# Low halves of split fp32 weights: an accumulating DMA in place of a VectorE subtraction, in a two-layer streaming encoder

## The chip, the cores and the metric

The kernel runs on one core of a Trainium2 chip. The metric is device time in microseconds (us) of one execution, as the median of several runs of the same program; less is better. Engines are called PE (TensorE), DVE (VectorE), ACT (ScalarE), POOL (GpSimd) and SP (SyncE, which only issues DMAs here). PEld is the weight load of TensorE.

## The reference

One step of an encoder with two layers, on 560 tokens (32 sample tokens, 16 meta tokens, 512 prompt tokens) of width 1024. Cut to what matters:

```python
def mixer_inputs(x, pos, lp):
    h = rmsnorm(x, lp["norm_g"])
    proj = jnp.einsum("btd,de->bte", h, lp["w_in"])      # 1024 -> 4688
    q, k, v, z_a, qi, ki, wi, u, v_m, o_m, z_m, ig, fg = split_cols(proj)
    ...

def layer_output(x, attn, z_a, h_m, c, o_m, z_m, lp):
    hn = rmsnorm(h_m, lp["head_norm_g"])
    branch_m = (jax.nn.sigmoid(o_m) * hn + lp["skip"] * c) * jax.nn.silu(z_m)
    branch_a = attn * jax.nn.silu(z_a)
    mixed = jnp.concatenate([branch_a, branch_m], axis=-1)
    return x + jnp.einsum("bte,ed->btd", mixed, lp["w_out"])
```

Between the two projections stand a sparse attention (an indexer scores all keys, the 128 best of a row are kept, 8 heads of 64 attend) and a chunkwise mLSTM (4 heads of 128, fed by a causal convolution). All is fp32, and the choice of the best keys makes it sensitive to the precision of the projections.

## The kernel before, in words

To reach fp32 precision with the faster fp32r matmul, each operand is split into a high half (the value rounded to fp32r) and a low half (the rest). A product is three matmuls: high by high, low by high, high by low.

The weights of a layer come in pieces of 128 or 256 columns, named by what they make: I and KI (indexer), U (convolution input), M (mLSTM values), Q, K, V, O, Z, G (gates), Y (output). `load_piece` brings one in as tiles of 128 x 512: two tiles for a piece of 128 columns, four for M and V, whose pieces have 256 columns. For each tile it issues a DMA from DRAM into `wraw` on SP's queue, copies that into the high half `whi` (on ACT, DVE or POOL, by the option `wh..`), and subtracts to get the low half `wlo` (DVE with option `wl..` 0, POOL with 2, by turns with 1). There are 180 tiles in the two layers; there are 3 buffers of `wraw` and 5 each of `whi` and `wlo`, used in turn, so tile n waits until the matmuls of tile n-5 have read theirs.

`mm_feat` multiplies a piece of 128 columns with all 560 tokens in two parts (304 and 256 columns); `mm_tok` does M and V, five blocks of tokens one after the other (blocks 4, 0, 1, 2, 3), each going through all four tiles. So the four tiles of an M or V piece come free only within its last block, and the next piece begins right after.

Instructions are emitted in the order of the lists `STEPS`, under priorities (`PR`, `SHIFT`), and a list scheduler that keeps its own estimate of time places them in each engine's queue. Every engine then works through its queue strictly in order: an instruction that waits holds up all behind it. POOL also does rotary products, convolution sums, the sums of squares at the start, small normaliser chains and a third of the softmax work; in the tables below its line L639 is the sum of squares and L641 and L642 the copies of the sample and meta tokens' columns.

The numbered lines in the profile belong to the kernel before: L490 is every plain DMA, L476 every copy by ACT, L513 the subtraction. `dap` describes a region of DRAM; the weights `w` stay there unchanged.

Of the kernel before, what the change touches and what calls it, by code (L numbers as in the profile page):

```python
# [9 lines left out]
F32 = mybir.dt.float32  # L10
# [4 lines left out]
OP = mybir.AluOpType  # L15

P = 128
# [33 lines left out]
WOFF = {}  # L51
# [4 lines left out]
WTOT = _o  # L56
# [381 lines left out]
def body(ctx, tc, nc, d):  # L438
# [6 lines left out]
    def T(tag, shape, dt=F32, name=None):  # L445
        tag = swap.get(tag, tag)
        cnt[tag] = cnt.get(tag, 0) + 1
        return pool.tile(shape, dt, tag=tag, bufs=BUFS.get(tag, 1), name=name or f"{tag}_{cnt[tag]}")
# [24 lines left out]
    act, dve, gps, pe = nc.scalar, nc.vector, nc.gpsimd, nc.tensor  # L473

    def acopy(out, in_, scale=1.0):
        return act.activation(out, in_, AF.Copy, scale=scale)  # L476
# [4 lines left out]
    def copy(site, l, out, in_, scale=1.0):  # L481
        o = OPT[f"{site}{l}"]
        if o == 0:
            return acopy(out, in_, scale)
        if isinstance(scale, float) and scale == 1.0:
            return (dve, gps)[o - 1].tensor_copy(out, in_)
        return (dve, gps)[o - 1].tensor_scalar(out, in_, scale, None, op0=OP.mult)

    def dma(out, in_):
        return nc.sync.dma_start(out, in_)  # L490

    def dap(t, off, ap):
        return bass.AP(tensor=t.tensor, offset=t.offset + off, ap=ap)
# [8 lines left out]
    def load_piece(l, name, base=1000):  # L502
        w = WIDTH[name]
        kk = 512 // w
        his, los = [], []
        with prio(l * 1000000 + base):
            for q in range(KT // kk):
                cut = lambda t: t[:, :kk * w].rearrange("p (k e) -> p k e", k=kk)
                raw, hi, lo = cut(T("wraw", [P, 512])), cut(T("whi", [P, 512], F32R)), cut(T("wlo", [P, 512], F32R))
                dma(raw, dap(d["w"], l * P * WTOT + WOFF[name] + q * kk * w, [[WTOT, P], [w, kk], [1, w]]))  # L510
                copy("wh" + name[0], l, hi, raw)
                o = OPT[f"wl{name[0]}{l}"]
                (gps if o == 2 or (o == 1 and q % 2) else dve).tensor_tensor(lo, raw, hi.bitcast(F32), op=OP.subtract)  # L513
                his.append(hi)
                los.append(lo)
        wtiles[l, name] = his, los, kk
# [144 lines left out]
    def layer(l, x_in, sums):  # L661
# [14 lines left out]
        for n in ("I0", "I1", "KI", "I2", "I3")[2 * (l == 0):]:  # L676
            load_piece(l, n)
# [207 lines left out]
        def conv(m):  # L885
            load_piece(l, f"U{m}")
            with prio(B + PR[l]["U"] + off[0]):
                u = T("gt", [P, 566])
                dma(u[:, 0:3], d["conv_in"][l, :, m, :])
                gps.memset(u[:, 35:38], 0.0)  # L890
                ps, ps1 = mm_feat(l, f"U{m}")
                with prio(B + PR[l]["D"]):
                    acopy(u[:, 3:35], ps[:, 0:32])
                    acopy(u[:, 38:310], ps[:, 32:304])
                    acopy(u[:, 310:566], ps1)
                gps.tensor_tensor(u[:, 3:35], u[:, 3:35], rrow[:, 0:32], op=OP.mult)
                E("us", l).tensor_tensor(u[:, 38:566], u[:, 38:566], rrow[:, 32:560], op=OP.mult)
                dma(d["sample_conv"][l, :, m, :], u[:, 32:35])
                dma(d["prompt_conv"][l, :, m, :], u[:, 563:566])
                y = T("gt", [P, 566])  # L900
                act.activation(y[:, :563], u[:, 0:563], AF.Identity, bias=sml[:, 16 + m:17 + m],
                               scale=sml[:, 4 * m:4 * m + 1])
                for i in range(1, 4):
                    if OPT[f"ut{i}{l}"]:
                        dve.scalar_tensor_tensor(y[:, :563], u[:, i:i + 563], sml[:, 4 * m + i:4 * m + i + 1], y[:, :563],
                                                 op0=OP.mult, op1=OP.add)
                        continue
                    tap = T("gt", [P, 566])
                    acopy(tap[:, :563], u[:, i:i + 563], sml[:, 4 * m + i:4 * m + i + 1])
                    gps.tensor_tensor(y[:, :563], y[:, :563], tap[:, :563], op=OP.add)  # L910
                act.activation(u[:, 0:563], y[:, :563], AF.Tanh, scale=0.5)
                dve.scalar_tensor_tensor(c2[:, m, 0:32], u[:, 0:32], 1.0, y[:, 0:32], op0=OP.add, op1=OP.mult)
                dve.scalar_tensor_tensor(c2[:, m, 32:560], u[:, 35:563], 1.0, y[:, 35:563], op0=OP.add, op1=OP.mult)
                dma(c2scr[l, m], c2[:, m, :])
# [3 lines left out]
        def proj_m(c):  # L918
            load_piece(l, f"M{c}")
            for j in ORDER:  # L920
                if c == 0:
                    v1[j] = T("v4" if j == 4 else "tok", [P, NTOK])[:, :516].rearrange("p (h e) -> p h e", e=129)
                    gps.memset(v1[j][:, :, 128:129], 1.0)
                mm_tok(l, f"M{c}", j, v1[j][:ROWS[j], 2 * c:2 * c + 2, 0:128], rc)
# [498 lines left out]
```

## Time and profile before

| what | value |
|---|---|
| median of 3 runs | 936.02 us (934.91 to 940.69) |
| the profiled execution's own time | 936.46 us |
| its span in the trace | 934.7 us |
| busy share PE / DVE / ACT / POOL | 92% / 79% / 46% / 51% |
| DMA: share of the 16 engines' time | 37% |
| mean granted TensorE clock | 0.968 |

Busy times are unions of an engine's instructions; DMA issues and waits are not counted in them. The chain that ended last is found by going back from the last instruction to whatever released it. Windows are stretches of the execution in us from the start of the span.

### The profile page before, as it was taken

To read this page: it belongs to the slowest core of one execution; us is meant where nothing else is said; L and a number is where in the kernel's file an instruction comes from. 1 tells how busy PE (TensorE), PEld (TensorE's weight loads), DVE (VectorE), ACT (ScalarE), POOL (GpSimd) and SP (SyncE) were. 2 spreads that over 40 slices of the span, in tenths; PEclk is the share of its full clock that TensorE was granted. 3 is DMA by queue.
4 is the path that set the end of the run, shared out by engine and by line. 5 is a ranking of instruction groups with operands and counts; after the bars stand their busy time and mean duration, and the time that the engine had idled before them with its cause. 6 is when DMAs were issued, how large, how long until landed. Compare 5 with 4: busy or idle time off the path is not lost.

```text
span 934.7 us, 18526 instructions
## 1 busy us (share of the span) xinstructions
PE 859.5 (92%) x6446; PEld 794.6 (85%) x6446; DVE 738.7 (79%) x1790; ACT 425.4 (46%) x1081; POOL 478.2 (51%) x825
## 2 busy tenths in 40 slices
PE   6877989999999999979999678999799999999998
PEld 5876889899888989858999667998699889888898
DVE  7699999899996865865757998898899886887531
ACT  5346735465555442454323666333355453243410
POOL 8466552474502223452824855248577765656411
PEclk9997999999999999979999979999799999999999
DMA  7432224443553232332643411334334642332152
GB/s 227 117 82 66 59 73 145 107 111 106 164 170 104 69 96 81 88 94 68 202 118 93 98 47 60 93 114 120 94 91 142 191 115 82 96 109 76 57 177 76
DMA packets 82158, 99.98 MB, mean 107 GB/s; under 512 B 16720, under 2 KB 44192, under 8 KB 82064
## 3 DMA queue, kind: packets, MB, share of 16 engines
q1 hardware_dynamic: 82064, 98.79, 37.0%
q8 instruction: 51, 0.84, 0.4%
q14 instruction: 43, 0.35, 0.1%
HBM read 72.19 MB, written 15.21 MB: 94 GB/s over the span
## 4 chain that ended last, share of the span: by engine, by line
PE 51%; DVE 24%; POOL 6%; DMA 6%; issue 6%; ACT 4%; SPq 2%; DVEq 0%; ACTq 0%; POOLq 0%
PE pj L559 10%; PE pj L561 10%; PE pj L560 10%; PE pv L1208 3%; DVE wlo L513 3%; PE sc L1171 2%; DVE wk L826 2%; SPq L490 2%; PE tp L1197 2%; DVE m L825 2%; PE pj L535 2%; PE pj L537 2%; PE pj L536 1%; PE pv L1209 1%; DMA fx<-kscr 1%
## 5 line engine op out<-in xcount | busy, mean ns | idle before, releaser
L559 PE MATMUL pj<-h,whi 128*128 128x304 f32 (+3 forms) x548 | 165.8, 305 | 14.9 <-ACT h L476 5.2
L561 PE MATMUL pj<-h,whi 128*128 128x256 f32 (+3 forms) x548 | 163.8, 301 | 2.7 <-DVE h L629 2.7
L560 PE MATMUL pj<-h,wlo 128*128 128x304 f32 (+3 forms) x548 | 163.5, 299 | 0.0
L476 ACT ACTIVATE whi<-wraw 128x512 fp32r<-128x512 f32 x130 | 80.2, 626 | 106.5 <-PE pj L561 63.4
L513 DVE TENSOR_TENSOR wlo<-wraw,whi 128x512 fp32r<-128x512 f32 x136 | 103.9, 768 | 26.7 <-ACT whi L476 26.3
L559 PEld LDWEIGHTS pj<-h,whi 128*128 128x128 f32 (+1 forms) x548 | 105.8, 194 | 19.4 <-ACT h L476 5.2
L561 PEld LDWEIGHTS pj<-h,whi 128*128 128x128 f32 (+1 forms) x548 | 105.4, 193 | 6.4 <-DVE h L629 5.0
L560 PEld LDWEIGHTS pj<-h,wlo 128*128 128x128 f32 (+1 forms) x548 | 106.1, 194 | 1.2 <-issue 0.8
L559 PE MATMUL pj<-at,whi 128*128 128x304 f32 (+2 forms) x346 | 104.8, 303 | 1.7 <-ACT tok L476 0.8
L561 PE MATMUL pj<-at,whi 128*128 128x304 f32 (+2 forms) x346 | 103.1, 299 | 0.0
L560 PE MATMUL pj<-at,wlo 128*128 128x304 f32 (+2 forms) x346 | 102.8, 297 | 0.0
L513 POOL TENSOR_TENSOR wlo<-wraw,whi 128x512 fp32r<-128x512 f32 x44 | 58.5, 1334 | 59.3 <-ACT whi L476 41.3
L559 PEld LDWEIGHTS pj<-at,whi 128*128 128x128 f32 (+1 forms) x346 | 66.6, 193 | 3.1 <-ACT tok L476 1.1
L825 DVE MAX8 m<-wk 96x8 f32<-96x560 f32 (+3 forms) x120 | 67.6, 563 | 1.6
L561 PEld LDWEIGHTS pj<-at,whi 128*128 128x128 f32 (+1 forms) x346 | 66.5, 192 | 0.6 <-issue 0.5
L560 PEld LDWEIGHTS pj<-at,wlo 128*128 128x128 f32 (+1 forms) x346 | 66.8, 193 | 0.1
L826 DVE MATCH_REPLACE8 wk<-m,wk 96x560 f32<-96x560 f32 (+3 forms) x120 | 65.8, 548 | 0.0
L1183 ACT ACTIVATE lg<-lg,sta,ssq 128x528 f32<-128x528 f32 (+3 forms) x64 | 42.4, 663 | 39.0 <-DVE sta L1182 35.9
L559 PE MATMUL pj<-tok,whi 128*128 128x304 f32 (+3 forms) x188 | 55.9, 297 | 0.0
L560 PE MATMUL pj<-tok,wlo 128*128 128x304 f32 (+3 forms) x188 | 55.6, 296 | 0.0
L561 PE MATMUL pj<-tok,whi 128*128 128x304 f32 (+3 forms) x188 | 55.4, 295 | 0.0
L1276 DVE TENSOR_TENSOR m<-pj,fr 128x304 f32<-128x304 f32 (+1 forms) x28 | 12.6, 449 | 45.7 <-PE pj L561 43.2
(386 smaller groups left out, 2584.9 us busy)
## 6 DMA issues: line engine op xcount, KB each, us to landing
wraw<-w SPq DMA_DIRECT2D x176, 256.0 KB, 2.8
fx<-fr SPq DMA_DIRECT2D x68, 70.0 KB, 2.5
m<-scratch SPq DMA_DIRECT2D x16, 256.0 KB, 4.0
fx<-tok SPq DMA_DIRECT2D x32, 70.0 KB, 2.4
c2scr<-ca SPq DMA_DIRECT2D x8, 280.0 KB, 2.2
k_out<-fr SPq DMA_DIRECT2D x8, 280.0 KB
gt<-c2scr SPq DMA_DIRECT2D x8, 280.0 KB, 2.6
m<-hmscr SPq DMA_DIRECT2D x8, 280.0 KB, 3.1
```

The lines of the kernel that those rows point to most:

```text
L476: return act.activation(out, in_, AF.Copy, scale=scale)
L490: return nc.sync.dma_start(out, in_)
L513: (gps if o == 2 or (o == 1 and q % 2) else dve).tensor_tensor(lo, raw, hi.bitcast(F32), op=OP.subtract)
L535: pe.matmul(ps[:R, :256], hh, wh, start=first, stop=False)
L537: pe.matmul(ps[:R, :256], hl, wh, start=False, stop=last)
L559: pe.matmul(o, wh, hh, start=(i == 0 and j == 0), stop=False)
L560: pe.matmul(o, wl, hh, start=False, stop=False)
L561: pe.matmul(o, wh, hl, start=False, stop=(i == 1 and j == 3))
L825: dve.max(m8[:R], src)
L826: dve.match_replace(out=wk[:R, :S], in_to_replace=m8[:R], in_values=src, imm_value=NEG)
L1183: act.activation(lg[:R, :S], lg[:R, :S], AF.Exp, bias=st[:R, 2:3], scale=qs, accum_out=st[:R, 3:4])
L1208: pe.matmul(o[s], vt[i][:, hs], pts[s][:, i * P:(i + 1) * P], start=(i == 0), stop=False)
```

## The change

For tiles whose low half DVE formed, the kernel now has ACT write the negated high half into `wlo`, and POOL then issue a DMA that reads the weights from DRAM a second time and adds them onto it in SBUF. Tiles whose low half POOL formed stay as they were. The lines behind the edit move down by 5.

```diff
@@ -507,10 +507,15 @@
             for q in range(KT // kk):
                 cut = lambda t: t[:, :kk * w].rearrange("p (k e) -> p k e", k=kk)
                 raw, hi, lo = cut(T("wraw", [P, 512])), cut(T("whi", [P, 512], F32R)), cut(T("wlo", [P, 512], F32R))
-                dma(raw, dap(d["w"], l * P * WTOT + WOFF[name] + q * kk * w, [[WTOT, P], [w, kk], [1, w]]))
+                src = dap(d["w"], l * P * WTOT + WOFF[name] + q * kk * w, [[WTOT, P], [w, kk], [1, w]])
+                dma(raw, src)
                 copy("wh" + name[0], l, hi, raw)
                 o = OPT[f"wl{name[0]}{l}"]
-                (gps if o == 2 or (o == 1 and q % 2) else dve).tensor_tensor(lo, raw, hi.bitcast(F32), op=OP.subtract)
+                if o == 2 or (o == 1 and q % 2):
+                    gps.tensor_tensor(lo, raw, hi.bitcast(F32), op=OP.subtract)
+                else:
+                    acopy(lo, hi.bitcast(F32), -1.0)
+                    gps.dma_start(out=lo, in_=src, accum_op=OP.add)
                 his.append(hi)
                 los.append(lo)
         wtiles[l, name] = his, los, kk
```

The scheduler sees other instructions, and its order moves on all engines. Three places follow; numbers behind a tile's name count the tiles of that name (the second is the compiler's own).

The first is POOL's queue at the start of the program, while the first indexer piece is loaded. Before:

```order
L639 TENSOR_TENSOR fx_1_123<-fx_1_123,lg_1_149 128x304
L641 COPY hc_1_140<-h_3_126 128x48
L642 COPY hc_1_140<-h_2_125 128x48
L642 COPY hc_1_140<-h_4_127 128x48
L641 COPY hc_1_140<-h_5_128 128x48
L639 TENSOR_TENSOR fx_1_123<-fx_1_123,lg_2_156 128x304
```

The same place after:

```order
L644 TENSOR_TENSOR fx_1_127<-fx_1_127,lg_1_153 128x304
L647 COPY hc_1_144<-h_2_129 128x48
L518 DMA wlo_1_86<-w 128x512
L644 TENSOR_TENSOR fx_1_127<-fx_1_127,lg_2_160 128x304
L646 COPY hc_1_144<-h_3_130 128x48
L647 COPY hc_1_144<-h_4_131 128x48
L646 COPY hc_1_144<-h_5_132 128x48
L518 DMA wlo_2_93<-w 128x512
```

The DMAs for the first two low halves stand between the sums of squares; PE's second matmul reads `wlo_1`.

The second is ACT's queue at the second M piece of the first layer, tiles 25 to 28 (`whi_26` needs the buffer of tile 21, which belongs to the first M piece). Before:

```order
L476 ACTIVATE whi_26_1797<-wraw_26_1796 128x512
L911 ACTIVATE gt_16_1365<-gt_17_1425 128x563
L476 ACTIVATE whi_27_1803<-wraw_27_1802 128x512
L476 ACTIVATE whi_28_1809<-wraw_28_1808 128x512
L476 ACTIVATE tok_8_1762<-pj_25_1764,smn_2_411 128x2x128
```

The same place after:

```order
L476 ACTIVATE whi_26_1822<-wraw_26_1821 128x512
L940 ACTIVATE m2_16_1511<-m2_16_1511,ta_1_681 48x48 x4
L886 ACTIVATE te_1_682<-tp_9_1500 48x8
L476 ACTIVATE whi_27_1829<-wraw_27_1828 128x512
L476 ACTIVATE wlo_26_1823<-whi_26_1822 128x512
L916 ACTIVATE gt_16_1385<-gt_17_1445 128x563
L476 ACTIVATE whi_28_1836<-wraw_28_1835 128x512
L476 ACTIVATE wlo_27_1830<-whi_27_1829 128x512
L476 ACTIVATE tok_8_1786<-pj_25_1788,smn_2_421 128x2x128
```

The negated copy into `wlo_26` stands behind four exponentials (L940), a small one and the next high half.

The third is POOL's queue at the same piece. Before:

```order
L910 TENSOR_TENSOR gt_17_1425<-gt_17_1425,gt_20_1433 128x563
L1051 TENSOR_TENSOR smk_2_1312<-smk_2_1312,smn_2_411 128x10
L543 TENSOR_SCALAR v4_1_1656<-v4_1_1656,smn_2_411 48x2x128
L486 COPY at_16_1345<-at_14_1337 64x48
L486 COPY at_16_1345<-at_15_1338 64x48
```

The same place after:

```order
L915 TENSOR_TENSOR gt_17_1445<-gt_17_1445,gt_20_1453 128x563
L518 DMA wlo_26_1823<-w 128x512
L518 DMA wlo_27_1830<-w 128x512
L518 DMA wlo_28_1837<-w 128x512
L518 DMA wlo_29_2025<-w 128x512
L486 COPY at_16_1363<-at_14_1355 64x48
L486 COPY at_16_1363<-at_15_1356 64x48
```

Four DMAs follow each other; the copies of the first keys and all of POOL's later work stand behind them.

On PE, between the last matmul that reads tile 21 and the first that reads `wlo_26`, stood 24 matmuls before; now 41 stand there.

## Rows read from the trace of the kernel before

**Rows 1.** Busy time, and shares of the chain that ended last (two rows of the page).

```profile
PE 859.5 (92%) x6446; PEld 794.6 (85%) x6446; DVE 738.7 (79%) x1790; ACT 425.4 (46%) x1081; POOL 478.2 (51%) x825
...
PE 51%; DVE 24%; POOL 6%; DMA 6%; issue 6%; ACT 4%; SPq 2%; DVEq 0%; ACTq 0%; POOLq 0%
```

**Rows 2.** Windows: stretch, length, busy us of each engine, clock, DMA share, GB/s.

```profile
0.00:23.00 23.00, 15.11 (x54) 12.71 (x55) 18.02 (x30) 12.15 (x25) 19.71 (x49) 1.00 0.75 230
...
47.00:117.00 70.00, 57.12 (x381) 50.67 (x380) 67.43 (x98) 44.28 (x95) 43.91 (x56) 0.93 0.26 69
117.00:260.00 143.00, 136.58 (x1088) 129.55 (x1086) 132.07 (x375) 74.34 (x206) 72.23 (x148) 0.98 0.43 121
...
515.00:585.00 70.00, 54.09 (x342) 48.01 (x341) 65.16 (x104) 44.77 (x97) 44.56 (x56) 0.90 0.26 68
...
796.00:913.00 117.00, 113.15 (x884) 104.10 (x883) 76.41 (x215) 40.80 (x101) 57.45 (x90) 1.00 0.34 102
```

**Rows 3.** The same windows, the subtraction L513 alone: DVE, then POOL.

```profile
47.00:117.00 70.00, 9.31 (x12) 0.00 (x0) 0.93 0.26 69
...
515.00:585.00 70.00, 8.95 (x10) 0.00 (x0) 0.90 0.26 68
```

**Rows 4.** Groups: line engine op out<-in, form, xcount | busy us, mean ns | idle before.

```profile
L476 ACT ACTIVATE whi<-wraw 128x512 fp32r<-128x512 f32 x130 | 80.2, 626 | 106.5 <-PE pj L561 63.4
L513 DVE TENSOR_TENSOR wlo<-wraw,whi 128x512 fp32r<-128x512 f32 x136 | 103.9, 768 | 26.7 <-ACT whi L476 26.3
...
L513 POOL TENSOR_TENSOR wlo<-wraw,whi 128x512 fp32r<-128x512 f32 x44 | 58.5, 1334 | 59.3 <-ACT whi L476 41.3
```

**Rows 5.** Tile view of `wlo`: who waited for it (us, times).

```profile
  PEld pj L532: 0.9, 2
...
  PE pj L532: 0.5, 2
```

**Rows 6.** Timeline at the start: start, us, engine, line, form.

```profile
4.70 0.69 DVE L513 TENSOR_TENSOR wlo<-wraw,whi 128x512 fp32r<-128x512 f32 x1 [4.70 <-ACT whi L476]
...
5.16 0.62 PE L559 MATMUL pj<-h,whi 128*128 128x304 f32 x1 [5.16 <-ACT h L476]
...
5.58 0.49 PE L560 MATMUL pj<-h,wlo 128*128 128x304 f32 x1
...
6.32 0.96 POOL L639 TENSOR_TENSOR fx<-fx,lg 128x304 f32<-128x304 f32 x1 [0.67 <-ACT h L476]
...
7.23 0.47 POOL L641 CAST hc<-h 128x48 fp32r<-128x48 f32 x1
```

**Rows 7.** DMAs: one weight tile's issue on SP (ns min/median/max), KB and us to landing.

```profile
L490 SPq DMA_DIRECT2D wraw<-w x180: 327/334/1377, 1.2 to 908.5; - x180
...
DMA to landing us min/median/max: 2.5/2.8/4.5
...
m<-scratch SPq DMA_DIRECT2D x16, 256.0 KB, 4.0
...
q1 hardware_dynamic: 82064, 98.79, 37.0%
```

**Rows 8.** Timelines of PE and ACT at the first layer's M pieces.

```profile
121.12 0.32 PE L532 MATMUL pj<-wlo,hc 128*48 128x256 f32 x1 [0.30 <-DVE wlo L513]
...
135.25 0.28 PE L536 MATMUL pj<-wlo,h 128*128 128x256 f32 x1
...
138.16 0.36 PE L532 MATMUL pj<-wlo,hc 128*48 128x256 f32 x1
...
135.33 0.63 ACT L476 ACTIVATE whi<-wraw 128x512 fp32r<-128x512 f32 x1 [0.22 <-PE pj L537]
...
140.99 1.01 ACT L935 ACTIVATE m<-m,ta 48x48 f32<-48x48 f32 x4
```

**Rows 9.** One short POOL copy in the stretches where DVE is full (ns min/median/max).

```profile
L756 POOL CAST at<-at x8: 209/722/776, 67.4 to 86.0; 128x32 fp32r<-128x32 f32 x8
```

## The prediction

> **What bounds the kernel now.** I read the page's busy shares and chain first, then the windows by stage, then the views of the low halves. PE is busy 92% of the span and carries half of the chain, DVE a quarter, POOL 6% [rows 1]. So the most that any change off PE can win is PE's idle time, 934.7 - 859.5 = 75 us. The windows show where it lies [rows 2]: in most stages PE works nearly all the time (113.2 of 117 us at 796 to 913), but in the two stretches where indexer scores and convolutions are made, at 47 to 117 and 515 to 585, PE idles 12.9 and 15.9 us while DVE works 67.4 and 65.2 of 70. There DVE is the bound, with ACT and POOL at 63% each. At the start PE idles 7.9 us of 23, waiting for input. At 117 to 260 PE (136.6 of 143) and DVE (132.1) are both near full.
>
> The low halves are not what PE waits for: in the whole run its projections and their weight loads waited for `wlo` 1.4 us [rows 5]. ACT's high halves wait for PE instead, 63.4 us in all [rows 4]: weights are prepared ahead, and a free buffer sets when.
>
> **The change part by part.** All sums are against the profiled execution, 936.46 us, which is 0.4 us above the median.
>
> Removed: 136 subtractions on DVE, 103.9 us [rows 4], of which 9.3 and 9.0 us lie in the two stretches that DVE bounds [rows 3]. The other 86 us lie beside a busy PE or in stages where both are near full.
>
> Added on ACT: 136 copies of the size of the high half's, 626 ns each [rows 4], 85 us. ACT goes from 425 to 510 us of 935, no bound by itself.
>
> Added on POOL: 136 DMA issues. No DMA is issued there before, so the trace has no price. SP's issue of the same tile takes 0.33 us [rows 7]; POOL's own subtraction of it 1.33 us [rows 4]. I take 1.0, nearer to POOL's row, because the work is done on POOL: 136 us, and POOL goes from 478 to about 614 us.
>
> Added on the DMA engines: 35 MB read again. The one queue moved 98.8 MB in 37.0% of the engines' time [rows 7], so 35 MB are 13 points, 26 if the destination is read as well. No stage but the first (75% busy [rows 2]) comes near full, so I cost the traffic at nothing there and count it in the landing. A plain tile lands 2.8 us after its issue, 4.5 at most, and the transfer of 256 KB with rereads takes 4.0 [rows 7]; I take 4.0, since this DMA handles its bytes twice. So from when POOL reaches the DMA to a usable low half I count 1.0 + 4.0 = 5 us, bounds 0.33 + 2.8 = 3.1 and 1.33 + 4.5 = 5.8, where one subtraction of 0.77 stood.
>
> *Where this is hidden.* In a piece of 128 columns a tile feeds 24 matmuls, one every 0.12 us [rows 8], some 3 us. With five buffers a tile is needed four tiles after its buffer came free, 11 us and more. High half, negation and DMA need 0.63 + 0.63 + 5 = 6.3 us. That cover costs nothing while the queues of ACT and POOL are prompt; without it each such tile would cost up to 5 us. No DMA tiles stand in layer 0's Y pieces (all on POOL); in layer 1's, POOL's half is used first.
>
> *The start: +4 us* (1 to 7). PE's second matmul reads the first low half at 5.58, right behind the subtraction at 4.70 to 5.39 [rows 6]. After, the order puts the DMA on POOL behind a sum of squares, which starts at 6.32 and takes 0.96, and a copy of 0.47 [rows 6]: reached at 7.8, landed at 12.8, so PE, in order, is 7.2 us late. It catches up what it idled there after its first matmul, 2.7 us of the 7.9 (its first matmul starts at 5.16 [rows 6]).
>
> *The M and V pieces: +12 us* (4 to 25). Their four tiles are freed only in the piece's last block of tokens, so the cover is thin. Before, the fourth tile of M0 was late already: PE waited for its subtraction [rows 8]. Tile 21 is read for the last time at 135.25, and `wlo_26` for the first time at 138.16 [rows 8]: 2.9 us for 24 matmuls. The scheduler has put 41 there now, 41 x 0.12 = 4.9 us. Against this stand, in ACT's new order, the high half 0.63, four exponentials 1.01 [rows 8], the next high half 0.63, the negation 0.63, and then 5 us: 7.9, and 8.3 with the small instruction and a start 0.1 us after the release. PE is short by 3.4 us. At M0's last tile, where 43 matmuls give 5.0 us and nothing stands between, it needs 0.63 + 0.63 + 5 = 6.3 and is short by 1.3. There are six such places (last tile of M0, M1 and V1, in each layer). I take 2 each, between the two: 12. With 3.1 us for the DMA they would nearly vanish; at 5.8 and a busier queue they double.
>
> *The stretches that DVE bounds: -10 us* (-20 to +5). At most 9.3 + 9.0 = 18.3 us go, and a couple more at 117 to 260. But 22 negations and DMAs go into the 140 us: ACT from 89 to 103 us, POOL from 88.5 to 110.5 [rows 2], and both stand in order, POOL behind waits for ACT. POOL's sums feed the convolution and the rotary products that DVE waits for. I let half of the gain through. The gain on DVE's sharing with POOL is unpriced and inside this range.
>
> *POOL's queue elsewhere: +7 us* (0 to 20). A DMA there waits for ACT's negation, and everything behind it waits too: the key copies and mLSTM products behind `wlo_26` to `wlo_29`, the small normaliser chains. The 44 subtractions on POOL already waited 41.3 us for the high half [rows 4], 0.94 each; at that rate 136 DMAs hold POOL 136 x 1.94 = 264 us, 28% of the time. The chain has 6% on POOL [rows 1], 56 us or some 40 pieces of 1.4; if each meets a held queue 28 times in 100 for half of 1.94 us, that is 11 us, of which I let 7 reach the end. Below nothing I see no mechanism.
>
> Sum: 936.5 + 4 + 12 - 10 + 7 = 949.5; I say 949, 1.4% slower.
>
> **What a page adds.** POOL's copy of 128 x 32 takes 209 ns at best and 722 in the median where DVE is full [rows 9]: POOL's work stretches 3.5 times there. The Trainium skill, page "SBUF — State Buffer", section "SBUF: two separate sides", says why this could strike the new DMAs: descriptors of a DMA issued from GpSimd are written by GpSimd's own cores, which are locked out while VectorE runs a copy in a mode that takes the port they share. Row and rule point the same way, against the change; no run here shows it for a DMA yet. It is the third rival below, whose price comes from the row.
>
> **The rivals.**
> Faster: the DMA is usable 3.1 us after POOL reaches it and DVE's relief comes through. The start costs 1, the six places 0.5 each, POOL's queue 2, the stretches give 20: 936.5 + 1 + 3 + 2 - 20 = 922. For it speaks that DVE is full there at 96% and 93% [rows 2]; against it, that POOL and ACT take up as much work as DVE loses. It decides where the first term in DVE's place (POOL) stays under some 75% busy there.
>
> No change: other matmuls fill the six places, as the order tries, and POOL's hold-ups fall where it idles: 936.5 + 4 + 3 - 10 + 3 = 937.
>
> Much slower: POOL becomes the bound in the two stretches. If an issue there stretches 3.5 times, 22 x 3.5 = 77 us join the 88.5 that POOL works: 165 of 140, so +25 in place of -10, and the M and V places, with issues 2.5 us later, cost 2.5 each more: 949.5 + 35 + 15 = 1000; with half of the stretching, 975. I price it at 982.
>
> The change doesn't do it: the DMA's rounding or form could make the compiler add instructions. The order shows 136 DMAs on POOL and no others, so 2 in 100, at about 949 too.
>
> **How the numbers follow.** Chances: forecast 0.46 (its own range 939 to 965), no change 0.24, faster 0.14, much slower 0.14, the last 0.02. The range of 8 in 10 must cut into both ends: 926 leaves about a tenth below, 976 a tenth above. A change within 1% (927.1 to 945.8 by the profiled time) can't be told from none. Faster: 0.12 of the rival and 0.01 of the no-change case, 0.13. Slower: the forecast's part above 945.8, 0.35, and 0.14, and 0.01 of the last: 0.50. The rest, 0.37, is the same.
>
> **What would show it.** Right: POOL gains 136 issues of about 1 us, DVE's busy time falls by some 100 us and ACT's rises by 85; PE's second matmul moves from 5.6 to 11 or later; PE's waits for a DMA onto `wlo` add up to 10 to 25 us, nearly all in M and V pieces; PE stays without such waits at 796 to 913. The two stretches shrink by less than 10 us together. Wrong: landing over 7 us, so that plain pieces wait too; an issue on POOL of 2 us or more; or DVE's stretches shrinking by their full 18 us. The weakest numbers are the two that no row prices, issue and landing: 1 us in their sum moves the M and V places by 6 us and POOL's queue by several.

## The result, and the profile after

The changed kernel takes 994.15 us (median of 4 runs, 992.53 to 1001.41) against 937.47 for the kernel before beside it: a ratio of 1.0616, 95% interval 1.0572 to 1.0661. The direction was as forecast; 949 us and the range up to 976 were not. The profiled execution took 1001.41 us, with a span of 999.6.

The page of the changed kernel, its rows on busy time, the two DMA queues (packets, MB, share of the engines' time) and the chain:

```profile
PE 879.6 (88%) x6446; PEld 814.8 (82%) x6446; DVE 665.5 (67%) x1654; ACT 499.6 (50%) x1217; POOL 567.0 (57%) x961
...
q1 hardware_dynamic: 82064, 98.79, 33.9%
q0 software_dynamic: 19584, 35.50, 22.9%
...
PE 53%; DVE 16%; DMA 13%; POOL 5%; issue 5%; ACT 4%; SPq 3%; DVEq 0%; POOLq 0%; ACTq 0%
```

Beside [rows 1], DVE has lost 73 us of busy time, ACT gained 74 and POOL 89. (POOL's 136 issues are counted as busy here, 961 instructions being 825 and 136; its other instructions take 471 us.) PE idles 120.0 us of the span (999.6 - 879.6) where it idled 75.2, and the same 6446 matmuls keep it busy 20.1 us longer: 44.8 + 20.1 are the 64.9 us by which the span grew. In the chain DVE's share fell by 8 points and DMA's rose from 6% to 13%; POOL's, which is where the new instructions stand, went down a point. That row misleads, as will be seen.

The new instructions, grouped (line engine op out<-in xcount | busy us, mean ns | idle before):

```profile
L518 POOL DMA_DIRECT2D wlo<-w x136 | 125.6, 957 | 107.6 <-ACT wlo L476 64.0
...
L476 ACT ACTIVATE wlo<-whi 128x512 fp32r<-128x512 f32 x136 | 84.0, 623 | 22.5 <-DVE whi L486 18.8
```

An issue takes 0.96 us, as assumed. But POOL also stands idle 107.6 us right before them, 64.0 of it for ACT's negation. The step holds the head of POOL's queue for 125.6 + 107.6 = 233 us.

The tile view of `wlo` after (first the groups, then who waited, us and times):

```profile
L565 PE MATMUL pj<-h,wlo x548: 276/297/622, 14.6 to 502.8; 128*128 128x304 f32 x89, 128*128 128x256 f32 x89, 128*108 128x256 f32 x3, 128*108 128x304 f32 x2
...
L518 POOL DMA_DIRECT2D wlo<-w x136: 589/884/1748, 7.8 to 979.4; - x136
...
  PE pj L565: 11.5, 2
...
  PE pj L537: 8.4, 8
...
DMA to landing us min/median/max: 3.8/4.9/9.2
```

POOL reaches the first DMA at 7.8 us, and PE's first matmul with a low half moves from 5.6 to 14.6. The landing is 4.9 us in the median. PE waits 11.5 us for two low halves of 128-column pieces (the first one is the start) and 8.4 us for eight of M and V. So the late low halves that the forecast priced are there, at about its price (19.9 us against 16), and the loss of 57 us is about three times as large. They are less than half of the 44.8 us by which PE's idle time grew: added up over all rows of the view of PE's waits, the time that ACT ended grew from 34 to 54 us, the time that POOL ended from 5 to 9.

The windows after, as [rows 2] (busy us of PE, PEld, DVE, ACT, POOL, clock, DMA share, GB/s; behind the first, the stages stand up to 65 us later in these stretches than before):

```profile
0.00:23.00 23.00, 9.01 (x45) 8.68 (x46) 17.18 (x25) 15.38 (x32) 20.46 (x52) 1.00 0.91 251
47.00:117.00 70.00, 57.64 (x369) 52.16 (x368) 56.73 (x76) 48.29 (x100) 48.20 (x64) 0.87 0.51 104
117.00:260.00 143.00, 123.55 (x910) 115.95 (x909) 123.07 (x353) 79.83 (x214) 79.87 (x155) 0.91 0.56 129
...
796.00:913.00 117.00, 110.56 (x815) 97.79 (x814) 69.55 (x213) 51.09 (x129) 75.24 (x141) 0.94 0.58 131
```

At 47 to 117 DVE is no longer full (56.73 of 70, before 67.43), and PE works no more for it (57.64, before 57.12, with 369 matmuls in place of 381). At 117 to 260 PE gets 910 matmuls done where it did 1088. POOL is nowhere near full: 48 of 70, 80 of 143.

### The profile page after: what moved, and what is told of

Its sections match the earlier page's. It is cut to its first block, busy times and chain, and to the rows that moved or that the text cites. A ratio compares the mean times of both kernels' runs of the same rounds, so it can differ in the third digit from the quotient of the medians.

```text
span 999.6 us, 18822 instructions
## 1 busy us (share of the span) xinstructions
PE 879.6 (88%) x6446; PEld 814.8 (82%) x6446; DVE 665.5 (67%) x1654; ACT 499.6 (50%) x1217; POOL 567.0 (57%) x961
## 3 DMA queue, kind: packets, MB, share of 16 engines
q1 hardware_dynamic: 82064, 98.79, 33.9%
q0 software_dynamic: 19584, 35.50, 22.9%
## 4 chain that ended last, share of the span: by engine, by line
PE 53%; DVE 16%; DMA 13%; POOL 5%; issue 5%; ACT 4%; SPq 3%; DVEq 0%; POOLq 0%; ACTq 0%
PE pj L564 10%; PE pj L565 10%; PE pj L566 10%; DMA m<-scratch 3%; SPq L490 3%; PE pv L1213 3%; PE pj L540 2%; DMA wlo<-w 2%; PE pj L542 2%; PE pj L541 2%; PE sc L1176 2%; DMA fx<-fr 2%; PE tp L1202 2%; DVE wk L831 2%; DMA fx<-kscr 2%
## 5 line engine op out<-in xcount | busy, mean ns | idle before, releaser
L564 PE MATMUL pj<-h,whi 128*128 128x304 f32 (+3 forms) x548 | 169.8, 311 | 22.3 <-DVE gt L1245 9.3
L518 POOL DMA_DIRECT2D wlo<-w x136 | 125.6, 957 | 107.6 <-ACT wlo L476 64.0
L565 PE MATMUL pj<-h,wlo 128*128 128x304 f32 (+2 forms) x548 | 165.3, 303 | 8.4 <-DMA wlo<-w 8.4
L566 PE MATMUL pj<-h,whi 128*128 128x256 f32 (+2 forms) x548 | 163.7, 302 | 0.1
L564 PEld LDWEIGHTS pj<-h,whi 128*128 128x128 f32 (+1 forms) x548 | 108.2, 198 | 27.0 <-DVE gt L1245 10.4
L565 PEld LDWEIGHTS pj<-h,wlo 128*128 128x128 f32 (+1 forms) x548 | 108.3, 198 | 9.8 <-DMA wlo<-w 8.8
L566 PEld LDWEIGHTS pj<-h,whi 128*128 128x128 f32 (+1 forms) x548 | 107.6, 197 | 0.9 <-DVE h L1260 0.3
L476 ACT ACTIVATE wlo<-whi 128x512 fp32r<-128x512 f32 x136 | 84.0, 623 | 22.5 <-DVE whi L486 18.8
L1188 ACT ACTIVATE lg<-lg,sta,ssq 128x144 f32<-128x144 f32 (+3 forms) x64 | 42.4, 663 | 50.2 <-DVE sta L1187 44.8
```

Of the source, the lines that this page charges most:

```text
L518: gps.dma_start(out=lo, in_=src, accum_op=OP.add)
L564: pe.matmul(o, wh, hh, start=(i == 0 and j == 0), stop=False)
L565: pe.matmul(o, wl, hh, start=False, stop=False)
L566: pe.matmul(o, wh, hl, start=False, stop=(i == 1 and j == 3))
L1188: act.activation(lg[:R, :S], lg[:R, :S], AF.Exp, bias=st[:R, 2:3], scale=qs, accum_out=st[:R, 3:4])
```

## The experiments

Theory 1 was the forecast's: late low halves at the start and at the M and V pieces, and PE's waits for them. Theory 2: the new step stands in order in the queues of ACT and POOL, and what they do behind it is late everywhere. Theory 3: the bytes of the second read. All times are medians, each ratio is against runs of the kernel before on the same chip (936.2 to 937.7 us), with its 95% interval. The scheduler makes a new order for each of these kernels; no run holds the order fixed.

### Where the loss lies: `mv_only`, `not_mv`

```diff
-                else:
+                elif not (name[0] in "MV"):                          # mv_only
+                elif not (name[0] not in "MV" and base != 0):        # not_mv
+                    dve.tensor_tensor(lo, raw, hi.bitcast(F32), op=OP.subtract)
+                else:
                     acopy(lo, hi.bitcast(F32), -1.0)
                     gps.dma_start(out=lo, in_=src, accum_op=OP.add)
```

`mv_only`:

> The accumulating DMA stays only for the M and V pieces (24 tiles of the 136 or so in question); all other tiles that it had get VectorE's subtraction back. Theory 1 (the M and V pieces receive late low halves, because four tiles come free at once and the new way takes some 6 us per tile): most of the loss outside the start is here, some 970 us, and PE waits for the DMA onto wlo stay at 8 us or more. Theory 2 (each DMA on POOL waits in order for ACT's negation, and everything that POOL and ACT do behind it is late, in proportion to the number of DMAs): 24 of 136 give about 10 us, 947 us. Theory 3 (the second read crowds the DMA engines): again in proportion, about 947 us.

Measured: 949.65 us, 1.0142 (1.0104 to 1.018). It has 32 such DMAs. What PE waits for in its trace:

```profile
PE pj L539 <- DMA wlo<-w: 16.7, 6, 4.9
```

`not_mv`:

> The complement: the accumulating DMA for all tiles that had it except those of the M and V pieces and of the first pieces of each layer (those loaded with base 0), which get VectorE's subtraction back. Theory 1: the start and the M and V pieces are mended, so about 940 us. Theories 2 and 3: most of the DMAs are still there and the loss with them, about 980 us.

Measured: 994.19 us, 1.0622 (1.058 to 1.0665), with 100 DMAs.

So the M and V pieces cost 13 us alone, where the forecast had 12 for them. The 13 also hold what these 32 tiles save DVE and what their issues hold up on POOL, so it is partly luck that the sizes agree. And mending them and the start wins nothing: the other 100 DMAs take 994 us by themselves. Theory 1 is right about the place of PE's waits, but they aren't the cause of the whole loss.

### Waits for low halves, and bytes: `nolat`, `narrow`, `nolat_narrow`

```diff
-                wh, wl = his[k // kk][:, k % kk], los[k // kk][:, k % kk]
+                wh, wl = his[k // kk][:, k % kk], his[k // kk][:, k % kk]   # nolat, nolat_narrow; likewise in mm_feat
...
-                    gps.dma_start(out=lo, in_=src, accum_op=OP.add)
+                    gps.dma_start(out=lo[:, 0, 0:16], in_=dap(d["w"], l * P * WTOT + WOFF[name] + q * kk * w, [[WTOT, P], [1, 16]]), accum_op=OP.add)   # narrow, nolat_narrow
```

`nolat`:

> As the changed kernel, with every negation and every accumulating DMA, but the matmuls take the high half of the weights where they took the low half, so no matmul waits for a low half (the product by the low half of the weights is left out of the result, the number of matmuls stays). Theory 1: the loss goes, about 945 us. Theory 2: the queues of ACT and POOL are as full as they were, about 980 us. Theory 3: the traffic is unchanged, about 980 us.

Measured: 991.24 us, 1.0592 (1.054 to 1.0645). With the bytes in place, taking away every wait for a low half wins 3 us of 57. In its trace the 19.9 us of waiting are gone, and PE's waits that DVE ends have grown from 33 to 54 us over all rows. So theory 1 alone can't be the cause.

`narrow`:

> As the changed kernel, with every negation, every issue on POOL and every wait, but the accumulating DMA moves only the first 16 elements of each row (8 KB in place of 256 KB; the rest of a low half stays the negated high half, so the projections are not the reference's). Theory 1: landing is somewhat earlier, about 980 us. Theory 2: queues as before, about 985 us. Theory 3 (traffic): the loss goes, about 945 us.

Measured: 979.12 us, 1.0456 (1.0407 to 1.0506). The step at POOL is as it was, and the landing shorter:

```profile
L518 POOL DMA_DIRECT2D wlo<-w x136: 589/882/1740, 7.9 to 956.1; - x136
...
DMA to landing us min/median/max: 2.2/3.0/5.3
```

`nolat_narrow` (its theories A and B are those of the section after the next):

> As the changed kernel, but the DMA moves only 8 KB in place of 256 KB, and the matmuls take the high half where they took the low half, so nobody waits for what the DMA brings (the product by the low halves is left out). What stays of the change is the negation on ACT and the issue on POOL with its wait. Theory A (POOL's queue): most of the loss stays, about 970 us. Theory B (bytes and landing): 915 us, as with ACT's copies alone.

Measured: 954.37 us, 1.0156 (1.0101 to 1.021). The step stands at POOL nearly as it did:

```profile
L518 POOL DMA_DIRECT2D wlo<-w x136 | 124.0, 932 | 91.0 <-ACT wlo L476 61.8 <-ACT pmx L476 8.6 <-DVE sta L1190 4.2
```

Without bytes and without anyone who waits for the result (the buffer is then also free sooner), the negation and the issue still cost 44 us over the kernel that has the negation alone (910.15, next section). That leaves 40 of the 84 us between that kernel and the changed one, and these don't divide. Bytes alone add 37 to the 954 us (`nolat`), the waits alone 25 (`narrow`), both together 40: either keeps most of the loss. Where low halves are waited for, the bytes are worth only 994 - 979 = 15. Theory 3 explains a part, not the larger one.

### Which queue: `act_only`, `pool_plain`, `neg_dve`, `free_lo`

```diff
-                    gps.dma_start(out=lo, in_=src, accum_op=OP.add)              # act_only: left out
...
-                    acopy(lo, hi.bitcast(F32), -1.0)                             # pool_plain: left out
-                    gps.dma_start(out=lo, in_=src, accum_op=OP.add)
+                    gps.dma_start(out=lo, in_=src.bitcast(F32R))
...
-                    acopy(lo, hi.bitcast(F32), -1.0)
+                    dve.tensor_scalar(lo, hi.bitcast(F32), -1.0, None, op0=OP.mult)   # neg_dve
...
-                (gps if o == 2 or (o == 1 and q % 2) else dve).tensor_tensor(lo, raw, hi.bitcast(F32), op=OP.subtract)
+                if o == 2 or (o == 1 and q % 2):                                 # free_lo, from the kernel before
+                    lo = cut(T("wlo", [P, 512], F32R))
+                    gps.tensor_tensor(lo, raw, hi.bitcast(F32), op=OP.subtract)
+                else:
+                    lo = hi
```

`act_only`:

> As the changed kernel, but without the accumulating DMAs: a low half is the negated high half and nothing is added to it (the projections are not the reference's). ACT has its 136 extra copies, DVE is rid of its 136 subtractions, POOL and the DMA engines are as before. The first runs left the waits for late low halves with little of the loss, the DMA's bytes with some 15 us of 58. Theory 2a (the rest is ACT's: its queue is in order and the copies hold up activations that PE waits for): about 970 us or more. Theory 2b (the rest is POOL's: issues that wait in order for ACT's copies hold up POOL's own products): about 935 us or less.

Measured: 910.15 us, 0.9738 (0.9692 to 0.9784). Its page:

```profile
PE 847.9 (93%) x6446; PEld 786.1 (87%) x6446; DVE 651.3 (72%) x1654; ACT 496.5 (55%) x1217; POOL 458.5 (51%) x825
```

ACT carries the same copies as in the changed kernel (496.5 us against 499.6), and the time is 26 us below the kernel before. So DVE's relief is real, ACT's 84 us are free, theory 2a falls, and what the DMAs cost is counted from here: 994 - 910 = 84 us. Of the 27 us by which the span is shorter, 12 are not idle time of PE: the same matmuls keep it busy 847.9 us in place of 859.5, at a mean granted clock of 0.979 (before 0.968).

`pool_plain`:

> As the changed kernel, but without ACT's negation: POOL issues a plain DMA of the same 256 KB into the low half (which then holds the weights themselves, so the projections are not the reference's). POOL has its 136 issues and the DMA engines their 35 MB; POOL never waits for ACT. Theory 2a (ACT): about 950 us, the 15 us of the bytes alone. Theory 2b, if POOL's waits for ACT are the cost: about 955; if the issues themselves are (1 us of POOL each): about 975.

Measured: 970.99 us, 1.036 (1.0301 to 1.042). A plain DMA's issue is shorter, and waits for PE's last read of the buffer in place of ACT:

```profile
L517 POOL DMA_DIRECT2D wlo<-w x136 | 78.4, 577 | 93.2 <-PE pj L565 61.5 <-PE pj L541 9.0 <-PE pj L564 6.6
```

Without ACT in it the step still costs 46 to 61 us (over `free_lo` or `act_only`), so it isn't the wait for ACT in particular.

`neg_dve`:

> As the changed kernel, but the negation is on DVE: ACT is as before the change, DVE has about as many operations as before, POOL has the 136 issues, each waiting for DVE. Theory 2a (ACT's queue): the loss falls to that of the bytes and of DVE's unchanged load, about 955 us. Theory 2b (POOL's issues wait in order for what makes the negated half): as the changed kernel or worse, 990 us.

Measured: 1032.0 us, 1.1021 (1.0991 to 1.1052), 38 us over the changed kernel: DVE's relief of 26 us is gone, and the step at POOL is still there. The other 12 us are not explained.

`free_lo`:

> The kernel before with DVE's 136 subtractions left out and nothing in their place: the matmuls take the high half where they took those low halves (the projections are not the reference's; 44 low halves still come from POOL). It shows what there was to win at most. If the stretches that DVE bounds were worth what their rows say, some 18 us and a little more at 117 to 260: about 915 us. If the end of the work is set by a chain over several engines instead and the new order costs as much as it wins: 930 to 940 us. Theory 2 in both forms says nothing on this run.

Measured: 925.34 us, 0.9889 (0.9869 to 0.9909). It has less work than `act_only` (no copies into `wlo`, no wait for them), and is 15 us slower:

```profile
PE 856.1 (93%) x6446; PEld 795.5 (86%) x6446; DVE 659.3 (71%) x1654; ACT 426.5 (46%) x1081; POOL 454.3 (49%) x825
```

The order that the scheduler made is another, and the granted clock is lower (0.965, `act_only` 0.979): PE's matmuls take 8 us more. Which of the two does it, or whether the clock follows the order, no run shows. I take 15 us as what a new order can bring here by chance, and read a difference of that size between two of these kernels (the 15 us of the bytes among them) with that doubt.

### POOL's time: `pool_work`, `pool_eighth`, `pool_full`, `pool_sub`, and `low_prio`

Theory A: the time at the head of POOL's queue costs, whatever stands there. Theory B: it is something of the DMA. The DMA is replaced by an addition on POOL, of three widths; `pool_sub` is the kernel before with all subtractions on POOL.

```diff
-                    gps.dma_start(out=lo, in_=src, accum_op=OP.add)
+                    gps.tensor_tensor(lo[:, :, :3 * w // 4], lo.bitcast(F32)[:, :, :3 * w // 4], raw[:, :, :3 * w // 4], op=OP.add)   # pool_work
+                    gps.tensor_tensor(lo[:, :, :w // 8], lo.bitcast(F32)[:, :, :w // 8], raw[:, :, :w // 8], op=OP.add)   # pool_eighth
+                    gps.tensor_tensor(lo, lo.bitcast(F32), raw, op=OP.add)       # pool_full
...
-                (gps if o == 2 or (o == 1 and q % 2) else dve).tensor_tensor(lo, raw, hi.bitcast(F32), op=OP.subtract)
+                gps.tensor_tensor(lo, raw, hi.bitcast(F32), op=OP.subtract)      # pool_sub
...
+                    with prio(l * 1000000 + PR[l][name[0]]):                     # low_prio
+                        gps.dma_start(out=lo, in_=src, accum_op=OP.add)
```

`pool_work`:

> As the changed kernel, with ACT's negations, but each accumulating DMA is replaced by work of POOL's own: POOL adds three quarters of the columns of the weights onto the negated half, some 1.0 us, about as long as an issue took (a quarter of each low half is left wrong). No second read, no landing. With ACT's copies alone the kernel took 910 us, with the DMAs 994. Theory A (what costs is the time that the new step stands at the head of POOL's queue, its 1 us and its wait for ACT, whatever the step is): about 975 us. Theory B (what costs belongs to a DMA: its bytes, its landing, the order made for it): about 920 us.

Measured: 984.07 us, 1.0497 (1.0455 to 1.0539). No DMA of the change is left, but most of its loss is.

`pool_eighth`:

> As the kernel in which POOL added three quarters of the columns (984 us), but it adds only one eighth, some 0.25 us, behind the same wait for ACT's negation (seven eighths of a low half are left without the weights). If what counts is POOL's own time at each tile, the loss over ACT's copies alone (74 us at 1.0 us a tile) falls to a quarter, 930 us; if it is the wait in POOL's queue for ACT, most stays, 960 us or more.

Measured: 945.32 us, 1.008 (1.0055 to 1.0105).

`pool_full`:

> The same with all columns, complete: ACT writes the negated high half and POOL adds the weights, 1.33 us a tile. If POOL's own time counts, the loss grows by a third, about 1010 us; if the wait does, it stays near 985 us.

Measured: 1002.33 us, 1.0691 (1.0665 to 1.0717).

`pool_sub`:

> The kernel before with all 180 subtractions on POOL, no negation and no DMA, complete. POOL's time per tile is that of the full addition, 1.33 us, but it waits one step of ACT less: if the time at POOL counts, about 1000 us; if the wait for ACT's second copy does, about 955 us.

Measured: 998.17 us, 1.0652 (1.0627 to 1.0677). It waits for one copy of ACT less than `pool_full` and is 4 us faster.

The step in the groups of POOL, by shape, for `pool_eighth`, `pool_work` and `pool_full` in turn:

```profile
L518 POOL TENSOR_TENSOR wlo<-wlo,wraw 128x64 fp32r<-128x64 f32 x132 | 51.0, 388 | 96.6 <-ACT wlo L476 76.3 <-PE pj L566 13.0 <-PE tp L1207 5.2
```

```profile
L518 POOL TENSOR_TENSOR wlo<-wlo,wraw 128x384 fp32r<-128x384 f32 x132 | 141.2, 1073 | 84.7 <-ACT wlo L476 76.6 <-PE pj L566 4.9 <-issue 1.2
```

```profile
L518 POOL TENSOR_TENSOR wlo<-wlo,wraw 128x512 fp32r<-128x512 f32 x132 | 177.6, 1351 | 100.1 <-ACT wlo L476 91.9 <-PE pj L566 3.3 <-DMA wraw<-w 2.4
```

The wait before the step is about the same in all three (85 to 100 us), its own time goes from 51 to 141 to 178 us, and the loss over `act_only` from 35 to 74 to 92 us. From the first to the last, 127 us more of POOL cost 57: 0.45 us for each us of POOL. Carried back to a step of no length, 35 - 0.45 x 51 = 12 us remain for waiting in order; both figures are estimates, since each kernel has an order of its own. `narrow`, whose DMAs move hardly a byte, lies on the same line: 126 us at POOL, 69 us over `act_only`. But `nolat_narrow`, with 124 us at POOL and nobody who reads the low half, lies 24 us below it. So a part of the 0.45 is paid only where PE needs the result, and 44 us is what the step in POOL's queue costs by itself. In the main theory A holds: a step of POOL's own, without a DMA, makes a loss of this size, and it grows with the step's length. Theory B is left with the bytes. By the line, POOL's own time at the step costs more than its wait for ACT.

`low_prio`:

> As the changed kernel, complete, but the accumulating DMA is given the priority of the piece's own matmuls in place of the highest, so that POOL's other work may be placed ahead of it. Theory A: POOL's products are held up less, 960 to 985 us, if low halves don't become late by it. Theory B: nothing is won, 990 us or more, since the low halves land later.

Measured: 999.39 us, 1.0647 (1.0605 to 1.0689). Nothing won: PE's idle time that ends with a DMA onto `wlo` is 23 us in its trace, 20 in the changed kernel's. The step holds POOL's queue for 123.2 + 114.1 us, as long as before, so this run says little about theory A.

### A version for the stretches alone: `u_only`

```diff
+                elif not (name[0] in "UK" and name not in ("K0", "K1", "K2", "K3")):
+                    dve.tensor_tensor(lo, raw, hi.bitcast(F32), op=OP.subtract)
```

> The kernel before with the accumulating DMA for the pieces of the convolution input and the indexer's keys alone (20 tiles, which are loaded around the stretches that DVE bounds), complete. A version that could beat both kernels: by both theories 20 DMAs cost some 12 us at the rate of the others (84 us for 136), and up to 18 us of DVE's work leaves the stretches: 925 to 945 us.

Measured: 932.26 us, 0.9936 (0.9906 to 0.9965), median of 10: 0.6% below the kernel before. Its windows:

```profile
47.00:117.00 70.00, 58.99 (x381) 52.66 (x380) 62.84 (x93) 48.98 (x102) 47.61 (x61) 0.90 0.45 96
515.00:585.00 70.00, 58.10 (x334) 52.93 (x335) 64.03 (x100) 41.07 (x91) 41.44 (x56) 0.81 0.31 71
```

PE does 381 matmuls in the first, as many as before, and 334 in the second, where it did 342: nothing is won where the version was meant to win. Its trace is that of an execution at 935.15 us (the ten took 926.97 to 935.9), 1.3 us shorter in span than the kernel before, so it can't show where the median's 5 us lie.

Where time goes in each kernel is seen by setting the same matmuls of two traces side by side, those of one line, names and shape paired in their order (another pairing moves single entries by up to 2 us). How many us later they start than before (median of those that start in 30 us of the kernel before):

| start before | after | `act_only` | `narrow` | `u_only` |
|---|---|---|---|---|
| 30 to 60 | 5.6 | -1.2 | 3.8 | 2.0 |
| 120 to 150 | 9.4 | -5.6 | 10.8 | 1.3 |
| 240 to 270 | 35.1 | -8.4 | 25.5 | 1.8 |
| 360 to 390 | 40.1 | -5.3 | 22.1 | 6.8 |
| 420 to 450 | 26.8 | -19.8 | 7.4 | -6.7 |
| 510 to 540 | 26.5 | -20.5 | 6.4 | -7.6 |
| 600 to 630 | 35.7 | -22.7 | 12.3 | -3.1 |
| 720 to 750 | 60.6 | -23.3 | 38.5 | 2.8 |
| 930 and later | 64.9 | -27.1 | 41.7 | -1.4 |

All four win some 14 us near 390, whatever else they lose. In `u_only`'s trace this step is the only large gain, and the rest uses it up again. It belongs to no work that was removed: `mv_only` has it too (18.6 at 360, 3.7 at 420), with all of DVE's subtractions there in place, while `not_mv` has not (16.2 and 13.3). It looks like a chance of the order; no run shows which instruction makes it.

## Why the prediction was wrong, step by step

**What bounds the kernel.** Held in part. DVE's subtractions are worth something (26 us by `act_only`), less than PE's idle time of 75. But that idle time is not the most that can be won: PE's busy time is not fixed either. It fell by 12 us in `act_only` and rose by 20 in the changed kernel, for the same matmuls.

**The prices of the parts.** Held: 0.96 us an issue (1.0 taken), 4.9 us to landing (4.0), ACT busier by 74 us at no cost. DVE's busy time fell by 73 us, not 100.

**The start, +4, and the M and V pieces, +12.** About right where they stand alone: matmuls at 30 to 60 us are 5.6 us late, and `mv_only` lost 13 us (with other things in it, as said). That nearly all waits would lie in M and V pieces did not come: 8.4 of the 19.9 us do. The mechanism can be read in the chain of the changed kernel at the second M piece:

```profile
147.02 0.86 POOL wlo L518
147.88 0.69 issue
...
148.60 6.26 DMA wlo<-w
...
154.90 1.09 PE pj L537 x4
```

In the whole they can't be added to the rest: with the waits for low halves gone (`nolat`) the kernel loses nearly the same, and PE waits for DVE instead.

**The stretches that DVE bounds, -10.** By themselves about right: `act_only` wins 6 us up to 120 to 150 and 2 more at 510 to 630, where the forecast let half of 18 through. Some 14 more of `act_only`'s 26 us come at the step near 390, which looks like chance. In the changed kernel no trace of it is left; the same matmuls are later at the end of both stretches than at their start.

**POOL's queue elsewhere, +7 (0 to 20).** This is the step that failed. `not_mv`, in which start and M and V pieces are mended, still loses 58 us. The forecast counted the 56 us that POOL has in the chain [rows 1] as the only time at which a hold-up of POOL matters, and let 28% of that meet half a wait. The time at the head of POOL's queue it had nearly right (264 us, measured 233). The runs show 44 us in place of the 7 for the step in POOL's queue by itself (`nolat_narrow` less `act_only`), and 0.45 us at the end for each us at POOL where PE also needs the result, on an engine that is busy 57% of the time. So the chain's share was the wrong price. What waits behind POOL's work shows in other rows, as in this wait of PE, before and after:

```profile
PE tp L1060 <- POOL smk L1051: 3.7, 2, 2.0
```

```profile
PE tp L1065 <- POOL smk L1056: 8.9, 2, 4.8
```

One passage of the changed kernel's chain shows another way:

```profile
194.72 0.37 POOL m L938
...
196.14 1.39 POOL fr L617
...
200.53 0.85 POOL wlo L518
...
201.43 0.64 POOL sm L596
...
202.43 0.12 POOL sm L598
202.56 5.67 DMA m<-scratch
...
208.24 4.90 DMA fx<-fr
```

The issue for a low half stands 0.85 us long between POOL's small normaliser steps. In this chain, whose links the profile infers, the transfers behind them are late by that and are booked under DMA. How much of the chain's DMA share of 13% (`m<-scratch` the largest of it, 3%) is of this kind isn't shown.

**The bytes, nothing.** Wrong too, by less: 15 us (`narrow`) to 37 (`nolat_narrow` against `nolat`), of which an order's chance of 15 us may be a part; with the waits for low halves they make up 40. By the page's rows the accumulating queue took 22.9% of 999.6 us for 35.5 MB, 6.4 us a MB, the plain one 33.9% for 98.79 MB, 3.4. POOL's waits for one other transfer rose too, before and after:

```profile
POOL m L933 <- DMA m<-scratch: 8.0, 4, 3.7
```

```profile
POOL m L938 <- DMA m<-scratch: 25.0, 8, 8.9
```

In `narrow` they are 13.4 us, and 12.0 in `pool_plain`, whose DMAs carry as many bytes as the changed kernel's without adding.

**The clock.** The sum had no term for it. The same matmuls took PE 20 us longer, at a mean granted clock of 0.935 (before 0.968, `act_only` 0.979); the windows at 47 to 117 and 117 to 260 have it at 0.87 and 0.91 where it was 0.93 and 0.98. No run varied the clock alone, so its share of the 0.45 isn't told apart, nor is it shown why it fell.

Put together from the runs: -26 (DVE's relief, ACT's copies free), +44 (the step in POOL's queue), +40 (the bytes and PE's waits for low halves, not told apart) make +58, where 57 was measured. These are differences of four kernels in a row, so that they add up proves nothing; the forecast had -10, +7 and +16 in their place.

**The rivals.** "Much slower" gave 975 to 1000 by POOL becoming the bound and issues stretched 3.5 times. The time came out there, by another way: POOL has 48.2 of 70 us in the first stretch, and the ten issues at 47 to 117 take 852 ns at least, 882 in the median, as in the whole run (884). The Trainium skill, page "SBUF — State Buffer", section "SBUF: two separate sides", has GpSimd locked out of writing descriptors while VectorE runs copies that take their shared port. The medians here don't show it, in `neg_dve` neither, where VectorE makes 136 copies of 128x512 more and the median issue takes 893 ns, the median landing 5.0 us (884 and 4.9 in the changed kernel). No row tells whether those copies take the port, and why single issues take up to 1748 ns isn't shown.

## What to carry to other kernels

Price what you put on an in-order engine by all that stands behind it in its queue, not by the engine's share of the chain and not by its idle time: here the step cost 44 us where the chain's share gave 7, on a POOL that idled nearly half of the time. A DMA issued from such an engine is an instruction of that engine, with the wait for its input in front. To see where a gain went, run the halves of the change alone: the half that was free (ACT's copies) and the half that wasn't (POOL's step) could not be told apart in the trace of the whole.

## What was not expected of the hardware

An issue on POOL takes 577 ns in the mean for a plain DMA of 256 KB and 957 ns for an accumulating one, with as many bytes; shrinking it to 8 KB leaves it at 947 ns. The accumulating queue kept the DMA engines 6.4 us a MB, the same queue with plain DMAs (`pool_plain`: 14.8% of 968.5 us for 35.5 MB) 4.0. And a kernel with less work (`free_lo`) was 15 us slower than one with 136 copies more, in another order and at a lower granted clock.
